# Diagonal blocks of a decayed Gram matrix stored once, and turned on chip for one of two scan directions

## The chip, the core and the metric

The kernel runs on one NeuronCore of a Trainium2 chip. A core has five engines that work at the same time: TensorE (PE in the profile; its weight loads are the row PEld), VectorE (DVE), ScalarE (ACT), GpSimd (POOL) and SyncE (SP), which here only issues DMAs. Each engine runs its own list of instructions strictly in order, and an instruction that waits for a semaphore holds up everything behind it on that engine. The metric is the device time of one whole execution in microseconds (us).

## The reference, cut to what matters

The program is one layer of a diffusion trunk over 2048 latent and 256 context tokens. An input projection feeds two token mixers: a gated delta rule that runs over the sequence in both directions (4 heads, key width 128, reference chunks of 64 tokens), and windowed attention. Both results are gated, projected, merged and projected once more.

The change touches the delta rule. For each chunk and head the reference builds a strictly lower triangular matrix and inverts one plus it:

```python
kb = kc * bc[..., None]
a_mat = jnp.where(strict, jnp.einsum('nbhik,nbhjk->nbhij', kb, kc) * decay, 0.0)
t_mat = lax.linalg.triangular_solve(a_mat, eye, left_side=True, lower=True, unit_diagonal=True)
...
o_f, s_f = _gdn_chunked(q, k, v, g[:, :, 0], beta[:, :, 0], s0_f, with_output)
o_b, s_b = _gdn_chunked(rev(q), rev(k), rev(v), rev(g[:, :, 1]), rev(beta[:, :, 1]), s0_b, with_output)
```

The second call runs on reversed tokens. So both directions use the same products of keys with keys, once in the lower and once in the upper triangle, each with its own decay and beta.

## The kernel before

The kernel works on 18 chunks of 128 tokens (2 of context, 16 latent; `LAT(j)` is chunk 2 + j). All big products are made of three matmuls each, since both operands are split into a high and a low half. The program is written in loops, and a planner orders the instructions of each engine by priority and by a simulation of the timeline; priority follows the order in which the program is written, except where `tc.high_priority` or `tc.issue_after` say otherwise. The order on each engine is then fixed: at run time a late DMA is waited for, and nothing overtakes it.

The stages, in the order of the profile:

1. Norm of the inputs and the small projections (to about 150 us).
2. `qkv(ORDER, ...)`: the projections v (m = 8 to 11), then k (m = 4 to 7), each in five segments: 256 context tokens and four times 512 latent tokens. `conv` applies the short convolution, and `finish` (L591) makes what the delta rule needs. For k, `finish` transposes the segment (L606), builds the Gram matrix of each chunk (L615), multiplies it with a table of decays `dt` that holds the forward decay in one triangle and the backward one in the other (L617, tile `p`), and spills blocks of 64 x 64 to DRAM through `spill_blocks` (L584). The backward direction (d = 1) reads `p` as it is. For the forward direction (d = 0) PE transposes each chunk of `p` against the identity (L629), ACT copies the result out of PSUM (L631, tile `pt`), and three more DMAs spill it. The tiles `p`, `pt`, the decays' `dt` and `qs` share the tag `o` with two buffers.
3. `qkv([0, 1, 2, 3], ...)`: the projection q, with the attention's queries beside it (from about 445 to 627 us).
4. `gates(range(24), (2, 3))`: 48 units of 24 matmuls, over the latter half of the tokens. Their order is fixed because the tiles `hh2` and `hh3` must be free before the scan can take their memory. Beside it, on DVE, `base` (L731) inverts the diagonal blocks of 8 heads-and-blocks times 8 chunks per direction at once: partition p holds one 64 x 64 block, forward blocks in partitions 0 to 63, backward ones in 64 to 127. It loads `N` (L745) and the betas `nb` (L744), multiplies (L748, L750), eliminates with 62 pairs of instructions per set (L758, L760), and stores (L770). There are two such sets: set 0 with the chunks that the scan needs first, set 1 with the others. A smaller one, `base4`, takes the last two chunks. `mod_gate` (L212) runs here too: 16 blocks of a weight are loaded into `wmg` (two buffers, L220), scaled by ACT (L221) and added up by POOL (L223).
5. `scan`: 18 steps, both directions side by side. `merge` (L999) loads the inverted diagonal blocks (`mx`, L1018) and the off-diagonal block (`moff`, L1020) of a chunk and completes the inverse of the whole 128 x 128 block with two rounds of 64 x 64 products. `chain` carries the state. Matmuls of `gates(range(24), (1, 0))` fill PE between them.
6. `attention`, `project` and the last projection (from about 1340 us to the end).

In `merge`, for the forward direction, the first product takes the block `moff` and the second half of the transposed inverse (L1037); DVE multiplies the result with beta into `y0` (L1041); the second product takes that and the first half of the inverse (L1044).

## Time and profile before

| what | us |
|---|---|
| median of 3 runs | 1994.18 (1990.22 to 1997.75) |
| the profiled execution | 1992.9 |
| its span, first to last instruction | 1991.2 |
| k segments, first Gram transposition to last (L629) | 300.5 to 435.9 |
| base, first to last elimination step (L758) | 647.2 to 949.8 |
| scan, first to last product with the inverse (L1115) | 920.7 to 1297.2 |

A row of the profile such as `L617 DVE TENSOR_TENSOR p<-gps,dtl x36: 423/690/693` names the line, the engine, the operation, the tile written and those read, the count, and the shortest, median and longest duration in ns. A row of the waits such as `DVE p L617 <- DMA dtl<-Dsp: 9.0, 5, 2.9` says that DVE stood for 9.0 us in all, 5 times, at most 2.9 us, in front of the instruction of line 617, and that a DMA ended it. `PEld` in front of a wait is the weight load's row; a `q` behind an engine's name is its sequencer, which also issues DMAs.

### The profile page before, as it was taken

What the parts mean: (1) busy time and instruction counts of PE and PEld (TensorE: products, weight loads), DVE (VectorE), ACT (ScalarE), POOL (GpSimd) and SP (SyncE); (2) the same over time, 40 slices, a digit from 0 to 9 for tenths busy, and PEclk for the clock granted to TensorE, in tenths of its full rate; (3) what the DMA queues carried; (4) which work ended last, traced back from release to release, by engine and by line L of the source; (5) the groups of instructions that cost most, each with busy time, mean ns of one, the idle gap of its engine ahead of it and who ended that gap; (6) DMA issues with size and microseconds to landing.
All of it is one profiled execution on the core that took longest, in us unless ns stands there. A gap on an engine that the chain in (4) does not pass through costs nothing. (4 is left out here: it accounts for less than half of the span.)

```text
span 1991.2 us, 32088 instructions
## 1 busy us (share of the span) xinstructions
PE 1917.4 (96%) x10947; PEld 1605.6 (81%) x10947; DVE 1502.1 (75%) x2869; ACT 802.6 (40%) x1994; POOL 692.1 (35%) x768
## 2 busy tenths in 40 slices
PE   7999999989999999999999999999989999999998
PEld 4888888779998787877888888788778887877786
DVE  6979766668776999999677776536686878747888
ACT  5755545554443323111222233225665656532221
POOL 2742211235542202004222234323555443420675
PEclk9999999999999999999999999999999999999999
DMA  7552226765547633528977877674455655455454
GB/s 263 173 142 87 91 89 161 195 157 175 151 134 196 170 106 116 145 89 237 230 232 225 240 212 207 178 216 146 143 176 171 185 161 164 119 173 190 141 169 135
DMA packets 387703, 333.12 MB, mean 167 GB/s; under 512 B 83992, under 2 KB 307536, under 8 KB 386900
## 3 DMA queue, kind: packets, MB, share of 16 engines
q1 hardware_dynamic: 352244, 288.60, 50.1%
q10 hardware_dynamic: 35296, 42.48, 6.1%
q8 instruction: 87, 1.43, 0.3%
q14 instruction: 76, 0.62, 0.1%
HBM read 220.28 MB, written 109.13 MB: 165 GB/s over the span
## 5 line engine op out<-in xcount | busy, mean ns | idle before, releaser
L535 PE MATMUL rps<-hh,wh 128*128 128x512 f32 x768 | 309.3, 403 | 3.7 <-DVE rt L829 2.5
L537 PE MATMUL rps<-hh,wl 128*128 128x512 f32 x768 | 307.6, 401 | 0.0
L536 PE MATMUL rps<-hl,wh 128*128 128x512 f32 x768 | 307.5, 400 | 0.0
L574 DVE SCALAR_TENSOR_TENSOR cacc<-y,cw,cacc 128x512 f32<-128x512 f32 (+1 forms) x224 | 164.0, 752 | 22.2 <-ACT cacc L572 18.3
L535 PEld LDWEIGHTS rps<-hh,wh 128*128 128x128 f32 x768 | 145.3, 189 | 39.4 <-DVE rt L829 3.3
L535 PE MATMUL lps<-hh,wh 128*128 128x512 f32 (+1 forms) x448 | 171.8, 384 | 0.3 <-ACT y L645 0.3
L536 PE MATMUL lps<-hl,wh 128*128 128x512 f32 (+1 forms) x448 | 171.5, 383 | 0.0
L537 PEld LDWEIGHTS rps<-hh,wl 128*128 128x128 f32 x768 | 145.2, 189 | 32.6
L536 PEld LDWEIGHTS rps<-hl,wh 128*128 128x128 f32 x768 | 145.5, 189 | 31.9
L537 PE MATMUL lps<-hh,wl 128*128 128x512 f32 (+1 forms) x448 | 171.0, 382 | 0.0
L961 DVE TENSOR_TENSOR pl<-pt,ph 128x512 fp32r<-128x512 f32 x156 | 105.4, 685 | 42.9 <-ACT ph L959 42.1
L959 ACT CAST ph<-pt 128x512 fp32r<-128x512 f32 x156 | 90.2, 585 | 110.2 <-PE pt L957 77.0
L827 ACT ACTIVATE rt<-rps 128x512 f32<-128x512 f32 x96 | 57.3, 597 | 185.0 <-PE rps L537 169.0
L933 DVE CUSTOM_DVE_ANT_0 pr<-sc,band,sk 128x640 f32<-128x640 f32 (+1 forms) x128 | 106.6, 862 | 32.1 <-PE sc L929 16.2
L943 POOL TENSOR_SCALAR pr<-pr,sm 128x640 f32<-128x640 f32 (+1 forms) x128 | 99.7, 802 | 56.5 <-DVE sm L941 39.3
L760 DVE TENSOR_TENSOR N<-N,btmp 128x62 f32<-128x62 f32 (+30 forms) x124 | 116.7, 941 | 3.0
L758 DVE TENSOR_TENSOR btmp<-N 128x62 f32<-128x62 f32 (+30 forms) x124 | 116.4, 939 | 3.1
L935 ACT ACTIVATE pr<-pr,sm 128x640 f32<-128x640 f32 (+1 forms) x128 | 104.0, 815 | 20.5 <-DVE sm L933 20.4
L246 DVE TENSOR_TENSOR wl<-wr,wh 128x512 fp32r<-128x512 f32 x120 | 92.4, 783 | 24.4 <-POOL wh L245 22.1
L1247 PE MATMUL pps<-yh,wph 128*128 128x512 f32 x256 | 105.6, 414 | 4.7 <-DVE tb L1258 2.5
L245 POOL TENSOR_SCALAR wh<-wr 128x512 fp32r<-128x512 f32 x72 | 48.8, 692 | 169.8 <-PE lps L536 97.1
L1248 PE MATMUL pps<-yl,wph 128*128 128x512 f32 x256 | 101.8, 399 | 0.0
(378 smaller groups left out, 5025.4 us busy)
## 6 DMA issues: line engine op xcount, KB each, us to landing
wr<-in_w_in_dram SPq DMA_DIRECT2D x120, 256.0 KB
kw<-Ksp SPq DMA_DIRECT2D x28, 384.0 KB
x<-vsp SPq DMA_DIRECT2D x36, 256.0 KB
k<-ksp SPq DMA_DIRECT2D x34, 256.0 KB
kT<-kTsp SPq DMA_DIRECT2D x34, 256.0 KB
wm<-in_w_mod_dram SPq DMA_DIRECT2D x16, 512.0 KB
xt<-in_x_dram SPq DMA_DIRECT2D x16, 512.0 KB
dtl<-Dsp SPq DMA_DIRECT2D x32, 256.0 KB
```

What stands on the lines that cost most here:

```text
L535: T.matmul(ps, lhsT=wh[:, k], rhs=xh[:, k], start=k == 0, stop=False)
L536: T.matmul(ps, lhsT=wh[:, k], rhs=xl[:, k], start=False, stop=False)
L537: T.matmul(ps, lhsT=wl[:, k], rhs=xh[:, k], start=False, stop=k == kt - 1)
L574: V.scalar_tensor_tensor(a, y[:, t:t + n], cw[:, m, t:t + 1], a, op0=ALU.mult, op1=ALU.add)
L758: V.tensor_tensor(tv, A[:, m + 1:, m].unsqueeze(2).to_broadcast([h1 + n, r, m]), A[:, m, 0:m].unsqueeze(1).to_broadcast([h1 + n, r, m]), o ...
L760: V.tensor_tensor(A[:, m + 1:, 0:m], A[:, m + 1:, 0:m], tv, op=ALU.add)
L933: V.tensor_tensor_reduce(s_, ps[:, o:768], band[:, b0:b0 + W + 256], -0.125, sk[:, 1, hd:hd + 1], ALU.add, ALU.min, sm[:, h, 1:2])
L935: S.activation(s_, s_, AF.Exp, scale=-1.0, bias=sm[:, h, 1:2], accum_out=sm[:, h, 2:3])
L943: G.tensor_scalar(p[:, h, :W + 256], p[:, h, :W + 256], sm[:, h, 3:4], 1.0, op0=ALU.mult, op1=ALU.mult)
L961: V.tensor_tensor(pl, pt, f32(ph), op=ALU.subtract)
L1247: T.matmul(ps, lhsT=wh[:, k, ms], rhs=hs[k], start=k == 0, stop=False)
L1248: T.matmul(ps, lhsT=wh[:, k, ms], rhs=ls[k], start=False, stop=False)
```

## The change

The diagonal blocks are stored once, as `p` has them, in one DRAM array `Nsp` in place of one per direction. The off-diagonal blocks of both directions are cut from `p` too, so the forward one is now stored the other way round and in partitions 0 to 63. PE's transposes of `p`, the copy `pt` and its spills go, except for the last two chunks of each head, whose forward diagonal blocks go to a small array `N4sp` for `base4`.

In front of the inversion the forward blocks are turned on chip. Set 0 loads all its forward blocks into a tile `u` (in the buffer that set 1's `N` takes afterwards), and three engines copy it with rows and columns exchanged: DVE 32 of the 64 columns, ACT 16, POOL 16. Set 1 is turned in eight pieces of 8 rows, each loaded into one buffer `ut` and copied by POOL. These loads and copies are now written in front of the gates of stage 4 and without the `issue_after` on the last convolution; the multiplications and the elimination stay where they were. `wmg` has one buffer in place of two.

In `merge` the forward direction's two products change places: DVE multiplies the loaded block with beta at once, the first product takes that and the first half of the inverse, ACT copies the result (in place of DVE's multiplication), and the second product takes it and the transposed half `W`.

```diff
-    Nsp = [dscr(f"Nsp{d}", [NC, H, 2, 64, 64]) for d in range(2)]
+    Nsp = dscr("Nsp", [NC, H, 2, 64, 64])
+    N4sp = dscr("N4sp", [2, H, 2, 64, 64])
...
-                wm = pool.tile([128, 512], F32, name="wmg", bufs=2)
+                wm = pool.tile([128, 512], F32, name="wmg", bufs=1)
...
-    def spill_blocks(d, t, c0, nn, h):
+    def spill_diag(dst, t, h):
         for b in range(2):
             r = slice(b * 64, b * 64 + 64)
-            dma(Nsp[d][c0:c0 + nn, h, b].rearrange("c r i -> r c i"), t[r, :, r])
-        dma(offsp[d][c0:c0 + nn, :, h].rearrange("c r i -> r c i"), t[64:128, :, 0:64])
+            dma(dst[:, h, b].rearrange("c r i -> r c i"), t[r, :, r])
+
+    def spill_blocks(t, c0, nn, h):
+        spill_diag(Nsp[c0:c0 + nn], t, h)
+        for d, (r, i) in enumerate(((slice(0, 64), slice(64, 128)), (slice(64, 128), slice(0, 64)))):
+            dma(offsp[d][c0:c0 + nn, :, h].rearrange("c r i -> r c i"), t[r, :, i])
...
-                spill_blocks(1, p, c0, nn, h)
+                spill_blocks(p, c0, nn, h)
...
-        if 4 <= m < 8:
-            pps = psum("gps", [128, 4, 128])
-            for j in range(nn):
-                T.transpose(pps[:, j], p[:, j], ident)
-            pt = pb.tile([128, 4, 128], F32, name="pt", tag="o")[:, :nn]
-            S.copy(pt, pps[:, :nn])
-            spill_blocks(0, pt, c0, nn, h)
+        if 4 <= m < 8 and c0 + nn == NC:
+            pps = psum("gps", [128, 2, 128])
+            for j in range(2):
+                T.transpose(pps[:, j], p[:, nn - 2 + j], ident)
+            pt = pb.tile([128, 4, 128], F32, name="pt", tag="o")[:, :2]
+            S.copy(pt, pps)
+            spill_diag(N4sp, pt, h)
...
+    def base_load(npool, fr, bk, turn):
+        N = npool.tile([128, 64, 64], F32, name="N")
+        nb = npool.tile([128, 64], F32, name="nb")
+        upper = [(slice(i0 * 8, i0 * 8 + 8 * k), Nsp[c:c + k].rearrange("c h b r i -> (c h b) r i")) for i0, c, k in runs(fr)]
+        turn(N, upper)
+        for d, chunks in ((0, fr), (1, bk)):
+            for i0, c, k in runs(chunks):
+                p0 = d * 64 + i0 * 8
+                dma(nb[p0:p0 + 8 * k], brT[c:c + k, d * 4:d * 4 + 4].rearrange("c h (b t) -> c (h b) t", b=2))
+                if d:
+                    dma(N[p0:p0 + 8 * k], Nsp[c:c + k].rearrange("c h b r i -> (c h b) r i"))
+        return N, nb
+
+    def turn_whole(pool):
+        def turn(N, upper):
+            u = pool.tile([128, 64, 64], F32, name="N")
+            for p, src in upper:
+                dma(u[p], src)
+            for copy, q in ((V.tensor_copy, slice(0, 32)), (S.copy, slice(32, 48)), (G.tensor_copy, slice(48, 64))):
+                copy(N[0:64, :, q], u[0:64, q].rearrange("p j r -> p r j"))
+        return turn
+
+    def turn_pieces(pool):
+        def turn(N, upper):
+            for q in range(0, 64, 8):
+                u = pool.tile([64, 8, 64], F32, name="ut", bufs=1)
+                for p, src in upper:
+                    dma(u[p], src[:, q:q + 8])
+                G.tensor_copy(N[0:64, :, q:q + 8], u.rearrange("p j r -> p r j"))
+        return turn
...
-    def base(si, npool, pool, fr, bk):
+    def base(si, N, nb, pool, fr, bk):
...
-            dma(N[p0:p0 + 16], Nsp[d][c:c + 2].rearrange("c h b r i -> (c h b) r i"))
+            dma(N[p0:p0 + 16], (N4sp, Nsp[c:c + 2])[d].rearrange("c h b r i -> (c h b) r i"))
...
     with tc.tile_pool(name="gate", bufs=1, reuse_waits="tile") as gp:
+        prepared = [base_load(bs, *SETS[0], turn_whole(bs2)), base_load(bs2, *SETS[1], turn_pieces(gp))]
         gates(list(range(24)), (2, 3), behind(4, mod_gate(gp, ones)), by_act=True)
...
         with tc.issue_after(last_conv[0].ins):
-            for _ in base(si, np_, bs2, fr, bk):
+            for _ in base(si, *prepared[si], bs2, fr, bk):
                 pass
...
-            dma(off[64:128], offsp[d][c])
+            r = slice(d * 64, d * 64 + 64)
+            dma(off[r], offsp[d][c])
...
         y0, y1 = offs[0], pool.tile([128, H, 64], F32, name="my1")
+        V.tensor_tensor(y0[0:64], y0[0:64], brb[0][0:64], op=ALU.mult)
...
-        in_step([lambda h: T.matmul(yps[0][0:64, h, 0:64], lhsT=offs[0][64:128, h], rhs=W[64:128, h, 64:128],
+        in_step([lambda h: T.matmul(yps[0][0:64, h, 0:64], lhsT=y0[0:64, h], rhs=Xs[0][0:64, h, 0:64],
                                     start=True, stop=True),
...
-        V.tensor_tensor(y0[0:64], yps[0][0:64, :, 0:64], brb[0][0:64], op=ALU.mult)
+        S.copy(y0[64:128], yps[0][0:64, :, 0:64])
...
-        in_step([lambda h: T.matmul(eps_[0][0:64, h, 0:64], lhsT=Xs[0][0:64, h, 0:64], rhs=y0[0:64, h],
+        in_step([lambda h: T.matmul(eps_[0][0:64, h, 0:64], lhsT=y0[64:128, h], rhs=W[64:128, h, 64:128],
                                     start=True, stop=True),
```

33 lines of the change are left out of this document (11 added, 22 removed).

## The prediction, made before the change was run

> **What bounds the kernel now.** I read the busy times of the engines by stage first.
>
> ```profile
> core 0: us, PE busy (x) PEld busy (x) DVE busy (x) ACT busy (x) POOL busy (x), PEclk, DMA share, GB/s
> 300.00:350.00 50.00, 50.00 (x286) 42.63 (x285) 32.76 (x60) 27.51 (x92) 4.99 (x4) 1.00 0.65 161
> 350.00:400.00 50.00, 47.57 (x277) 39.82 (x276) 34.77 (x67) 25.45 (x86) 13.88 (x16) 1.00 0.78 198
> 400.00:445.00 45.00, 39.19 (x272) 34.91 (x270) 31.58 (x72) 24.19 (x81) 14.31 (x13) 1.00 0.61 155
> 445.00:627.00 182.00, 181.25 (x1257) 165.18 (x1256) 137.70 (x318) 83.54 (x251) 87.43 (x103) 1.00 0.51 156
> 627.00:896.00 269.00, 266.48 (x1135) 212.10 (x1134) 247.52 (x292) 63.58 (x108) 34.20 (x26) 0.99 0.49 134
> 896.00:1300.00 404.00, 395.52 (x2891) 343.42 (x2889) 292.69 (x691) 104.41 (x338) 135.07 (x206) 0.99 0.77 220
> ```
>
> PE is the bound in each of these stages, at full clock in the first four rows. In 350 to 445 us it stands for 2.43 + 5.81 = 8.2 us. In the stage of the gates and of `base` (627 to 896) it stands for 2.5 us of 269; DVE is nearly full too (247.5), so I look at who needs DVE there:
>
> ```profile
> L758 DVE TENSOR_TENSOR btmp<-N x124: 212/1022/1828, 647.2 to 949.8; 128x62 f32<-128x62 f32 x4, 128x122 f32<-128x122 f32 x4, 128x180 f32<-128x180 f32 x4, 128x236 f32<-128x236 f32 x4
> L770 SPq DMA_DIRECT2D Xsp<-N x4: 512/548/590, 803.7 to 953.6; - x4
> L1018 SPq DMA_DIRECT2D mx<-Xsp x64: 573/607/2607, 898.3 to 1196.0; - x64
> ```
>
> `base` stores set 0 at 803.7 and the scan first reads such a block at 898.3: 94 us to spare. Set 1 is stored at 953.6 and first needed at step 8 of the scan, whose 18 steps fill the 404 us of the last row above (22 us each): at 898 + 8 x 22 = 1074. So the inversion is not on the path; the scan begins when the 48 gate units are through. Their pace:
>
> ```profile
> 859.73 0.39 PE L535 MATMUL rps<-hh,wh 128*128 128x512 f32 x1
> ...
> 886.33 0.39 PE L535 MATMUL rps<-hh,wh 128*128 128x512 f32 x1
> ```
>
> 114 matmuls lie between these starts, 26.60 / 114 = 0.233 us each; 48 x 24 x 0.233 = 268 us is the whole stage. Whatever PE saves before 627 us moves everything behind it forward by as much, as long as nothing new stops PE.
>
> **The change, part by part.** *The transposes in the k stage.*
>
> ```profile
> L629 PE MATMUL gps<-ident,p x72: 270/272/303, 300.7 to 435.9; 128*128 128x128 f32 x72
> 327.70 0.60 PE L629 MATMUL gps<-ident,p 128*128 128x128 f32 x4
> PE gps L629 <- DVE p L617: 2.7, 4, 1.5
> PE gps L629 <- DVE y L647: 2.2, 1, 2.2
> PE tmps L373 <- ACT y L645: 1.7, 1, 1.7
> PE gps L629 <- DVE y L650: 0.8, 1, 0.8
> ```
>
> Of 72 transposes 8 stay (two per head): 64 go. Four of them take 0.60 us with 0.27 for the last alone, so each follows the other by 0.11 us: 64 x 0.11 = 7.0 us of PE. In front of them PE stood for 2.7 + 2.2 + 0.8 = 5.7 us: it reaches the transpose before DVE has made `p`, and in order it cannot pass. With the transposes gone nothing on PE reads `p` in this stage except the 8 that stay. Bounds 0 (the next matmul waits for the same lateness) to 5.7; I take 4, nearer to the upper end, because what is next is mostly a dense product that needs only weights and `hh`.
>
> ACT and the queues of the same step:
>
> ```profile
> L631 ACT COPY pt<-gps x20: 372/584/610, 301.6 to 436.9; 128x512 f32<-128x512 f32 x16, 128x256 f32<-128x256 f32 x4
> ACT pt L631 <- DMA offsp<-pt: 8.1, 5, 3.6
> L588 SPq DMA_DIRECT2D Nsp<-pt x40: 574/598/818, 302.0 to 438.6; - x40
> L617 DVE TENSOR_TENSOR p<-gps,dtl x36: 423/690/693, 296.3 to 627.7; 128x512 f32<-128x512 f32 x32, 128x256 f32<-128x256 f32 x4
>   DMA dtl<-Dsp: 23.1, 18
> DMA packets 58987, 26.52 MB, mean 166 GB/s; under 512 B 31064, under 2 KB 56279, under 8 KB 58972
> ```
>
> ACT loses 16 of 20 copies (16 x 0.58 = 9.3 us) and most of an 8.1 us wait for the buffer of `pt`. Behind that copy on ACT stand the copies `y` that free PSUM for PE; the 1.7 us that PE waited for `y` L645 are of this kind: bounds 0 to 1.7, I take 1. SP loses 40 spills of diagonal blocks and gains 8, 32 x 0.60 = 19 us of its issue time; the off-diagonal ones stay 40. DVE waited 23.1 us for decays `dtl` queued behind those spills. All this feeds DVE and ACT, which are not full here, so beyond the 1 us I count nothing, and the rest stands as the rival of a larger gain. Sum of the k stage: 7.0 + 4 + 1 = 12, bounds 7.0 to 7.0 + 8.2 (all of PE's idle time) = 15.2.
>
> *The turning of set 0.*
>
> ```profile
> DVE N L748 <- DMA N<-Nsp: 6.1, 1, 6.1
> DVE N L750 <- DMA N<-Nsp: 6.1, 2, 4.2
> L748 DVE TENSOR_TENSOR N<-N,nb x8: 416/810/1210, 634.5 to 655.0; 64x256 f32<-64x256 f32 x2, 64x512 f32<-64x512 f32 x2, 64x768 f32<-64x768 f32 x2, 64x1024 f32<-64x1024 f32 x2
> L750 DVE TENSOR_TENSOR N<-N,nb x8: 422/821/1227, 643.6 to 660.3; 64x256 f32<-64x256 f32 x2, 64x512 f32<-64x512 f32 x2, 64x768 f32<-64x768 f32 x2, 64x1024 f32<-64x1024 f32 x2
> L1042 ACT COPY my<-myp x18: 369/369/371, 912.2 to 1285.4; 64x256 f32<-64x256 f32 x18
> L1014 POOL COPY mx<-x x8: 620/629/992, 1223.1 to 1274.8; 64x256 f32<-64x256 f32 x8
> L245 POOL TENSOR_SCALAR wh<-wr 128x512 fp32r<-128x512 f32 x72 | 48.8, 692 | 169.8 <-PE lps L536 97.1 <-PE rps L536 56.9 <-DMA wr<-in_w_in_dram 15.2
> ```
>
> DVE copies 2048 elements per partition; 1024 took 1.21 us, so about 2.4. ACT: 256 took 0.37 and 512 took 0.58, so 1024 about 1.0. POOL: the only strided copy here takes 0.63 for 256, so 1024 takes 2.5. Forward blocks landed by 634.5 and were multiplied; DVE then stood until 643.6 for the backward ones. Turning (2.5) and the four multiplications (3.3) end at 640.3, inside that wait. Cost 0; if the cover were gone, 2.5 us on a chain with 94 us to spare. No bound of it reaches PE unless an eviction (`rt`, L829) behind a waiting copy is late by more than the three PSUM banks hold, 3 x 24 x 0.233 = 17 us.
>
> *The eight pieces of set 1 and the single buffer of `wmg`.* All are on SP, in front of or between the loads of gate weights (L241) and the stores.
>
> ```profile
> SPq L220 <- POOL gacc L223: 14.2, 6, 6.9
> SPq L241 <- DVE wl L246: 12.4, 7, 4.7
> ACT wh L243 <- DMA wr<-in_w_in_dram: 8.8, 4, 5.4
> 674.88 2.09 SPq L220 DMA_DIRECT2D wmg<-in_w_mod_dram  x2
> 679.49 0.72 ACT L221 ACTIVATE wmg<-wmg,silc 128x512 f32<-128x512 f32 x1 [3.92 <-DMA wmg<-in_w_mod_dram]
> ```
>
> The second of those two issues ends at 676.97 and ACT has the data at 679.49: 2.5 us to land. A piece of half that size lands, is copied by POOL (512 elements strided: 2 x 0.63 = 1.26 us) and only then frees `ut` for the next load: 0.34 + 2.5 + 1.26 = 4.1 us, eight times 33 us if SP stands at each. A gate unit pair covers 48 x 0.233 = 11.2 us, and weights are loaded one pair ahead. So the bounds for the pieces are 0 and 33 - 11 = 22 us of PE. I take 1, because SP already stood 14.2 + 12.4 us in this stretch and ACT 8.8 us for weights while PE lost 2.5 us. `wmg` with one buffer makes 16 rounds of 2.5 + 0.7 + 1.5 us, which 269 us hold easily; its waits go with the same 1 us.
>
> [...]
>
> *The merge.* Matmuls stay as many. DVE's multiplication (L1041) moves in front, ACT gets a copy of 0.37 us per step (18 x 0.37 = 6.6 us, on an engine busy 104 of 404 us: 0). The new wait: DVE now reads `moff` straight from its DMA, with the state's instructions queued behind it, and PE waits for those.
>
> ```profile
> L1041 DVE TENSOR_TENSOR moff<-myp,br x18: 405/406/410, 913.7 to 1286.6; 64x256 f32<-64x256 f32 x18
> 1040.20 0.47 SPq L1020 DMA_DIRECT2D moff<-offsp  x1
> 1045.00 0.49 PE L1027 MATMUL mtp<-ident,mx 128*128 128x128 f32 x3
>   DMA x<-vsp: 31.2, 18
> ```
>
> The nearest row is POOL's first use of `x` (L1102), which waited 31.2 us over 18 times: upper bound 31, lower bound 0, or -1.5 where PE no longer waits for L1041. I take 1: `moff` is issued 4.8 us ahead of the transposes in the quoted step, and it is not needed sooner.
>
> **The sum.** 1992.9 - 12 + 1 + 1 = 1982.9 us, against the profiled execution, which lies 1.3 us under the median shown. I say 1983.
>
> **Rivals.** *The gain is lost on the way.* PE's next instruction waits for the same DVE and ACT work, and a planner that orders everything anew gives some back. For it: DVE is 65 to 70% busy in the k stage and PE's idle time there is mixed. Against it: in 300 to 350 us PE is never idle, so its own work is what ends last. Only some of the 7.0 us then arrive: 1992.9 - 3 = 1990.
>
> *A larger gain.* All 8.2 us of idle time go: 1992.9 - 15.2 = 1978. For it: SP's 19 us, ACT's 17 and the spills' packets, of which 32 x 256 = 8192 go (64 rows of 4 chunks each), out of 31064 small ones. Against: part of the waits is for `conv`, which stays. [...]
>
> *SP is held by the pieces, and the gates' weights come late* (slower). Place: 630 to 700 us, SP in order, L241 behind the loads into single buffers. Price: 22 us of PE for the pieces, up to 36 with three rounds of `wmg` (3 x 4.7 us) among them; I take 25, 1992.9 - 12 + 1 + 25 = 2007. It decides from the point where a weight load is issued over 11.2 us late. For it: 33 us of holding in a stretch that already has 27. Against: the planner knows of these waits and only their excess over its own times counts.
>
> **How the numbers follow.** What a measurement here can tell from no change is about 0.5%, 10 us: under 1984.2 is faster, over 2004.2 slower. Chances: forecast 0.50 (its own range 1977 to 1989), gain lost 0.26, larger gain 0.13, slower 0.11. Of the forecast's half, 0.31 lies under 1984.2; with 0.13 of the larger gain and 0.02 of the lost one, faster has 0.46. The slower rival and the tail of the merge's wait leave 0.11 over 2004; same has 0.43. The range that holds 8 in 10: 1975 (upper bound of the k stage, the merge's -1.5 and some spread) to 1997 (gain lost, with part of the pieces' hold).
>
> **What would show it.** In the profile after: L629's successor with 8 matmuls; PE without waits for `p` in the k stage and the q stage beginning some 12 us sooner; the gates' stage still about 269 us long, with PE idle under 4 us; the base's first elimination at the same distance from the stage's beginning; few us of DVE waiting for `moff`. Wrong if the k stage is shorter by less than 7 us, if PE waits for weights between the first gates and the pieces' last copy, or if the scan is longer than 404 us by more than a few.

## The result and the profile after

The changed kernel takes 2015.75 us (median of 4 runs, 2013.49 to 2017.79), the kernel before 1994.99 us beside it (1990.22 to 1997.75): 1.0106 times as long, with a 95% interval of 1.0082 to 1.0131. The forecast was 1983 us. The profiled execution took 2017.79 us, its span is 2016.1 us, 24.9 us more than the 1991.2 of the span before.

Busy time by stage, kernel after (columns as in the prediction; the stages begin where the same work begins, so the borders differ from those before):

```profile
300.00:350.00 50.00, 50.00 (x276) 42.51 (x274) 32.28 (x62) 26.02 (x90) 6.18 (x6) 1.00 0.60 152
350.00:400.00 50.00, 45.45 (x269) 38.65 (x268) 35.82 (x70) 25.43 (x89) 14.79 (x15) 1.00 0.71 183
400.00:439.00 39.00, 34.01 (x226) 30.00 (x225) 29.19 (x69) 19.28 (x68) 14.76 (x13) 1.00 0.62 165
439.00:621.00 182.00, 181.21 (x1254) 164.99 (x1254) 136.61 (x317) 82.25 (x249) 86.28 (x101) 1.00 0.50 154
621.00:902.00 281.00, 270.52 (x1136) 214.44 (x1135) 252.44 (x286) 64.89 (x110) 51.23 (x34) 0.98 0.47 128
902.00:1320.00 418.00, 404.01 (x2882) 345.75 (x2881) 298.29 (x697) 110.39 (x349) 133.94 (x208) 0.99 0.74 210
```

The stage from 439 us on begins 6 us sooner, not 12. PE stands for 10.5 us of the gates' row, where it stood for 2.5, and the scan's row is 14 us longer than the 404 of before.

For a table of stages I take three marks that every kernel has: the first matmul of a gate, the scan's first load of an inverted block (`mx<-Xsp`, issued when the 48 gate units are through), and attention's last score. Instructions by tile, columns: duration min/median/max in ns, first and last start in us. Kernel after:

```profile
L536 PE MATMUL rps<-hh,wh x768: 388/394/793, 611.5 to 1444.7; 128*128 128x512 f32 x192
L1045 SPq DMA_DIRECT2D mx<-Xsp x64: 573/605/2642, 904.7 to 1221.8; - x64
L954 PE MATMUL sc<-kw,qT x128: 276/336/525, 1367.9 to 1763.5; 128*128 128x384 f32 x112, 128*128 128x256 f32 x16
```

The same, kernel before (its `mx<-Xsp` row, 898.3, stands in the prediction):

```profile
L535 PE MATMUL rps<-hh,wh x768: 388/394/789, 617.0 to 1418.5; 128*128 128x512 f32 x192
L927 PE MATMUL sc<-kw,qT x128: 276/336/522, 1342.8 to 1738.7; 128*128 128x384 f32 x112, 128*128 128x256 f32 x16
```

| us | gates begin | gates' stage | scan and attention | rest | span |
|---|---|---|---|---|---|
| before | 617.0 | 281.3 | 840.4 | 252.5 | 1991.2 |
| after | 611.5 | 293.2 | 858.8 | 252.6 | 2016.1 |
| difference | -5.5 | +11.9 | +18.4 | +0.1 | +24.9 |

So the k stage gave 5.5 us; the gates' stage took 11.9 back and the scan with attention 18.4 more. Scan and attention are kept together because both plans put the remaining gate units beside them, some more in the one, some more in the other; the sum of work is the same.

**The k stage.** Waits of PE between 290 and 450 us, and the transposes that stay, kernel after:

```profile
PE zt L612 <- DVE cacc L577: 5.4, 4, 2.1
PE gps L635 <- DVE p L623: 2.4, 2, 1.8
L635 PE MATMUL gps<-ident,p x8: 270/272/328, 328.0 to 428.8; 128*128 128x128 f32 x8
```

The 64 transposes are gone. The 5.7 us in front of them are not: PE now waits 5.4 us for the convolution's result (`cacc`) one step sooner, and 2.4 us in front of two of the eight transposes that stay.

**The gates' stage.** Timeline of the loads (SP) and of DVE, kernel after: start, duration, engine, line, and in brackets the idle time before it and what ended it.

```profile
620.94 0.35 SPq L722 DMA_DIRECT2D N<-Nsp  x1
623.93 0.45 SPq L722 DMA_DIRECT2D N<-Nsp  x1
629.68 0.60 SPq L730 DMA_DIRECT2D N<-Nsp  x1
```

```profile
633.31 2.09 DVE L776 TENSOR_TENSOR N<-N,nb 64x768 f32<-64x768 f32 x2
635.43 0.69 DVE L855 SCALAR_TENSOR_TENSOR rt<-rt,rps 128x512 f32<-128x512 f32 x1
643.20 2.10 DVE L732 COPY N<-N 64x2048 f32<-64x2048 f32 x1 [7.08 <-DMA N<-Nsp]
645.33 3.59 DVE L774 TENSOR_TENSOR N<-N,nb 64x256 f32<-64x256 f32 x3
648.84 3.38 DVE L247 TENSOR_TENSOR wl<-wr,wh 128x512 fp32r<-128x512 f32 x2
652.15 0.67 DVE L855 SCALAR_TENSOR_TENSOR rt<-rt,rps 128x512 f32<-128x512 f32 x1
```

The planner puts the load of the blocks to be turned (L730, tile `u`) behind both loads of the backward blocks. It is issued at 629.68 and landed at 643.2, when the backward blocks had been through their multiplications for 8 us. DVE stands before it for 7.1 us, then turns, multiplies, and makes `wl`; the next eviction of a gate (`rt`, L855) comes 16.7 us after the one before. Waits in this stage (611 to 902 us), kernel after: engine, tile, line, what was waited for, us in total, times, longest.

```profile
PE rps L536 <- DVE rt L855: 10.5, 4, 4.2
...
ACT wmg L222 <- DMA wmg<-in_w_mod_dram: 57.9, 14, 9.9
...
ACT wh L244 <- DMA wr<-in_w_in_dram: 15.2, 6, 4.9
ACT N L732 <- DMA N<-Nsp: 9.6, 1, 9.6
```

The same rows of PE and ACT, kernel before (617 to 896 us):

```profile
PE rps L535 <- DVE rt L829: 2.5, 1, 2.5
ACT wmg L221 <- DMA wmg<-in_w_mod_dram: 20.7, 10, 4.1
```

PE waits 8.0 us more for evictions than before, two thirds of the stage's 11.9 us. Most of the rest goes with the granted clock, by an estimate from the records. Busy time and clock between 650 and 700 us, kernel before and kernel after:

```profile
650.00:700.00 50.00, 47.48 (x197) 37.69 (x196) 47.32 (x60) 14.83 (x25) 11.45 (x9) 0.97 0.56 156
650.00:700.00 50.00, 40.85 (x154) 31.80 (x155) 48.26 (x58) 11.80 (x22) 22.22 (x16) 0.91 0.52 146
```

Behind the one pause of PE in the stage before (2.5 us) the trace has 3.4 us at half clock (a granted share of 0.50). After, there are three such pieces, from 653.7, 681.0 and 698.0 us, behind pauses of 4.2, 2.9 and 2.7 us. In the first of them the gates' matmuls follow each other by 0.43 us, behind it by 0.23:

```profile
654.55 0.63 PE L538 MATMUL rps<-hh,wl 128*128 128x512 f32 x1
654.97 0.63 PE L536 MATMUL rps<-hh,wh 128*128 128x512 f32 x1
...
657.33 0.39 PE L536 MATMUL rps<-hh,wh 128*128 128x512 f32 x1
657.56 0.40 PE L537 MATMUL rps<-hl,wh 128*128 128x512 f32 x1
```

If half of each piece is lost, that is 5.1 us in place of 1.7 (an estimate from these records). With the 8.0 us it makes 11.4 of the 11.9. ACT, which evicts and casts weights here, now stands 57.9 us for `wmg` and 9.6 for `u`; the detail above is of the first pause, and what share each cause has in the other two is not shown.

**Scan and attention.** DVE waits in the scan (895 to 1330 us), kernel after; the kernel before has no such row:

```profile
DVE moff L1061 <- DMA moff<-offsp: 22.4, 10, 8.6
```

This row made my first theory: the merge costs through DVE, which stands in front of a late load with the scan's instructions behind it.

### The profile page after: what moved, and what is told of

Read it like the earlier page. It is cut to its first block, busy times and chain, and to the rows that moved or that the text cites. A ratio compares the mean times of both kernels' runs of the same rounds, so it can differ in the third digit from the quotient of the medians.

```text
span 2016.1 us, 31836 instructions
## 1 busy us (share of the span) xinstructions
PE 1923.0 (95%) x10883; PEld 1603.5 (80%) x10883; DVE 1511.3 (75%) x2870; ACT 803.8 (40%) x1997; POOL 706.9 (35%) x777
## 5 line engine op out<-in xcount | busy, mean ns | idle before, releaser
L536 PE MATMUL rps<-hh,wh 128*128 128x512 f32 x768 | 310.6, 404 | 12.7 <-DVE rt L855 10.5
L1278 PE MATMUL pps<-yh,wpl 128*128 128x512 f32 x256 | 100.9, 396 | 0.0
```

Source lines behind the costliest of these rows:

```text
L536: T.matmul(ps, lhsT=wh[:, k], rhs=xh[:, k], start=k == 0, stop=False)
L1278: T.matmul(ps, lhsT=wl[:, k, ms], rhs=hs[k], start=False, stop=k == 3)
```

## The experiments

All comparisons are with the kernel before on the same chip, which took 1987.7 to 1990.8 us in these sessions. Stages by the marks above, from one profiled execution each; the ratio decides on the whole and the stages tell where. The profiled execution lies within 6 us of its kernel's median, but for e4 (11.5 us under it) and e15 (7.8 us over it); the kernel before's, 1992.9 us, is 2 to 5 us over the medians of these sessions. So a few us in one row for a stage mean little.

| kernel | gates begin | gates' stage | scan and attention | rest | ratio of times |
|---|---|---|---|---|---|
| before | 617.0 | 281.3 | 840.4 | 252.5 | 1 |
| after | 611.5 | 293.2 | 858.8 | 252.6 | 1.0106 |
| e1 merge alone | 623.2 | 281.6 | 844.5 | 256.5 | 1.0093 [1.0066, 1.0120] |
| e4 turning alone | 618.0 | 290.8 | 839.5 | 251.0 | 1.0111 [1.0071, 1.0150] |
| e5 k stage alone | 611.5 | 285.0 | 846.8 | 252.9 | 1.0046 [1.0023, 1.0070] |
| e9 one `wmg` buffer alone | 616.7 | 287.6 | 848.9 | 255.6 | 1.0105 [1.0076, 1.0133] |
| e3 after, no turning | 611.6 | 287.1 | 851.7 | 251.5 | 1.0100 [1.0075, 1.0125] |
| e6 after, old merge | 613.6 | 292.9 | 855.8 | 250.8 | 1.0129 [1.0102, 1.0155] |
| e2 after, product held | 612.5 | 293.0 | 858.8 | 250.1 | 1.0155 [1.0126, 1.0183] |
| e7 after, `moff` early | 611.6 | 292.9 | 859.5 | 253.8 | 1.0166 [1.0140, 1.0191] |
| e12 e7, product held | 611.8 | 291.9 | 844.9 | 252.3 | 1.0087 [1.0062, 1.0112] |
| e16 e1, early and held | 623.0 | 282.9 | 844.9 | 253.8 | 1.0090 [1.0069, 1.0111] |
| e8 turned by POOL | 610.0 | 289.4 | 859.3 | 255.3 | 1.0150 [1.0125, 1.0175] |
| e11 turned by ACT | 612.2 | 294.8 | 853.4 | 254.6 | 1.0137 [1.0115, 1.0160] |
| e13 two `wmg` buffers | 611.9 | 300.1 | 855.5 | 253.9 | 1.0187 [1.0160, 1.0213] |
| e14 inversion held | 612.3 | 293.6 | 859.2 | 255.7 | 1.0157 [1.0132, 1.0183] |
| e15 e12, e13, e14 together | 613.8 | 297.0 | 858.5 | 252.5 | 1.0141 [1.0113, 1.0169] |
| e10 transposes twice | 620.1 | 281.4 | 838.0 | 252.6 | 1.0032 [1.0015, 1.0050] |
| e17 inversion late | 616.9 | 290.7 | 850.2 | 250.3 | 1.0102 [1.0061, 1.0142] |
| e18 directions swapped | 618.8 | 281.8 | 853.8 | 251.2 | 1.0083 [1.0059, 1.0108] |

### One part at a time

**e1, the merge alone.** The kernel before with the edits in `merge`, and both off-diagonal blocks spilled from `p`:

```diff
-        dma(offsp[d][c0:c0 + nn, :, h]..., t[64:128, :, 0:64])
+        if d:
+            for dd, (r, i) in enumerate(((slice(0, 64), slice(64, 128)), (slice(64, 128), slice(0, 64)))):
+                dma(offsp[dd][c0:c0 + nn, :, h]..., t[r, :, i])
```

> The kernel before with the new merge alone: the forward off-diagonal block is cut from p instead of pt, DVE multiplies it with beta as soon as it is loaded, ACT copies the first product. Transposes, pt and the inversion stay as before. Theory A (the scan is longer because DVE waits for the DMA of moff at the front of each merge): the stretch from the first to the last product with the inverse grows from 372 us by 10 to 20 us, and the time is 2005 to 2015. Rival B (the scan is longer only because its start and the second inversion set came late, so DVE is shared for longer): the stretch stays at 372 and the time within 4 us of before, 1995.

2007.46 us, inside theory A's range. But the place is not A's: of the span's 14.6 us only 4.1 lie in scan and attention, although DVE waits for `moff` more than in the kernel after, and the stretch that theory A names grew by 6 us (927.8 to 1306.1, in place of 920.9 to 1292.9), not by 10 to 20; 6.2 lie ahead of the gates and 4.0 behind attention, which I did not follow up. Its row, kernel e1:

```profile
DVE moff L1036 <- DMA moff<-offsp: 26.5, 12, 5.1
```

**e2, the product held behind the first transposes.**

```diff
-        V.tensor_tensor(y0[0:64], y0[0:64], brb[0][0:64], op=ALU.mult)
+        with tc.issue_after(first_tp.ins):
+            V.tensor_tensor(y0[0:64], y0[0:64], brb[0][0:64], op=ALU.mult)
```

> The changed kernel, with DVE's multiplication of moff in merge held back until PE has made the transposes of the forward block, by when moff has landed. Theory A: DVE's wait of 22 us for moff goes, the scan's stretch falls from 392 to 372 to 380 us, the time from 2016 to about 2000. Rival B: the stretch stays near 392 and the time near 2015.

2018.72 us, but nothing was tested: DVE's product already stood behind these transposes in the order, every engine's list is the same as in the kernel after, and the wait stayed (20.7 us). It serves as a second measurement of the kernel after. The two stages agree within 0.2 us; the ratios, 1.0106 and 1.0155, show that two sessions can differ by 0.5% with the same lists.

**e3, the kernel after without turning**: the forward blocks are loaded as stored, so what is inverted for them is the transposed block.

```diff
-        turn(N, upper)
+        for p, src in upper:
+            dma(N[p], src)
```

> The changed kernel without the turning: the forward blocks are loaded straight into N, in the stored orientation (so the forward inverses are those of other matrices); everything else as changed, the merge too. Theory C (the turning holds DVE in front of the evictions of the gates' stage): PE's waits for rt in 611 to 903 us go from 10.5 to under 3 us, the stage from 292 to about 281 us, the time from 2016 to about 2004. Rival D (the stage is longer because the loads were moved in front of the gates, turned or not): the stage stays within 3 us of the changed kernel's.

2008.44 us, between the two. The gates' stage gives 6.1 of its 11.9 us back, scan and attention 7.1 of 18.4, in an execution 4.9 us under the median. PE's waits for `rt` stay at 7.1 us, where theory C had under 3. The rest is there without any turning.

**e4, turning alone.** The kernel before with `base_load`, `turn_whole`, `turn_pieces` and one buffer for `wmg`; the k stage and the merge are the old ones.

```diff
-        N = npool.tile([128, 64, 64], F32, name="N")
+        prepared = [base_load(bs, *SETS[0], turn_whole(bs2)), base_load(bs2, *SETS[1], turn_pieces(gp))]
...
-                wm = pool.tile([128, 512], F32, name="wmg", bufs=2)
+                wm = pool.tile([128, 512], F32, name="wmg", bufs=1)
```

> The kernel before with the turning alone: the forward blocks are read from the backward direction's array and turned as in the change, with the loads in front of the gates and one buffer for wmg; transposes, pt, spills and merge as before. Theory C: the gates' stage is 10 to 13 us longer and the time 2005 to 2008. Rival E (the turning hurts only because the k stage ended earlier and the loads met other transfers): the stage is under 4 us longer and the time under 2000.

2012.58 us; the profiled execution was its fastest, 2001.07. The gates' stage has +9.5 us, scan and attention nothing (-0.9). Theory C has the place right and is too low in time; where the other 11.5 us of the median lie, no trace shows.

**e5, the k stage alone.**

```diff
-        turn(N, upper)
+        for p, src in upper:
+            dma(N[p], src)
...
-            dma(off[r], offsp[d][c])
+            dma(off[64:128], offsp[d][c])
```

This is the kernel after with the first edit of e3, the merge of before, and two buffers for `wmg`. The loads for the inversion still stand in front of the gates, as in the kernel after.

> The change's k stage alone (transposes, copies and spills gone, two extra diagonal chunks stored turned, two buffers for wmg again). The turning is left out (the forward direction's diagonal blocks are inverted as they are stored) and the merge is the one of before, which here reads the untransposed off-diagonal blocks, so the output differs. Theory A (turning and merge are what costs): about 6 us faster than before, the 5.5 us by which the gates began sooner in the kernel after; gates' stage 279 us long, TensorE idle between gates and attention 42 to 44 us. Rival B (any new plan of the scan around the k stage's shorter work costs some 15 us, whatever the merge does): 2000 us or more, TensorE idle between gates and attention above 52 us.

1997.57 us, 9 us slower where theory A said 6 faster. The 5.5 us are gained, then 3.7 are lost in the gates' stage and 6.4 in scan and attention, whose code is the one of before. Rival B is too high with 2000, but right in kind: the loss needs neither the turning nor the merge. What of the 3.7 us comes from the moved loads is not shown.

**e6, the kernel after with the old merge.** Its turning and its `wmg` stay as they are.

```diff
-            dma(off[r], offsp[d][c])
+            dma(off[64:128], offsp[d][c])
...
-        V.tensor_tensor(y0[0:64], y0[0:64], brb[0][0:64], op=ALU.mult)
...
-        S.copy(y0[64:128], yps[0][0:64, :, 0:64])
+        V.tensor_tensor(y0[0:64], yps[0][0:64, :, 0:64], brb[0][0:64], op=ALU.mult)
```

> The kernel after with the merge of before in place of the new one (it reads the untransposed off-diagonal blocks, so the output differs). Theory A (the new merge costs 13 to 17 us of TensorE between gates and attention): 1998 to 2003 us, that idle time back at 42 to 44 us, gates' stage still 288 to 291 us long. Rival B (the turning costs as much as it did when made alone, 25 us, and the merge nothing on top): 2010 to 2016 us.

2014.08 us. Without the new merge scan and attention still take 855.8 us, 15.4 more than before. Theory A, that the merge is what the scan loses, falls here.

**e9, one buffer for `wmg`, and nothing else.**

```diff
-                wm = pool.tile([128, 512], F32, name="wmg", bufs=2)
+                wm = pool.tile([128, 512], F32, name="wmg", bufs=1)
```

> The kernel before with one buffer in place of two for wmg, and nothing else; no work is added or removed, but the planner then puts 22% of TensorE's matmuls from the scan on into another order. Theory P (what the merge and the scan lose is the price of another order of the scan, which any edit ahead of it can bring): 4 to 20 us slower, TensorE idle between gates and attention above 46 us in place of 42.4. Rival M (the order is worth nothing by itself, only the edited merge and the turning cost): within 4 us of before, idle time 41 to 45 us.

2012.01 us: this one word costs about as much as the whole change. ACT's row in the gates' stage, kernel e9:

```profile
ACT wmg L221 <- DMA wmg<-in_w_mod_dram: 49.5, 13, 11.4
```

Against 20.7 with two buffers: ACT stands at each round, with evictions and casts behind it. The gates' stage is 6.3 us longer, and PE waits 7.1 us for evictions there. The 8.5 us in scan and attention are as theory P says, since no instruction there has changed but its place.

### The wait for `moff`

**e7, the load a whole step sooner** (and the copied product in a tile of its own):

```diff
+    def load_off(pool, cs):
+        off = pool.tile([128, H, 64], F32, name="moff", bufs=3)
...
+                if st + 2 < NC:
+                    offs.append(load_off(pool, [orders[d][st + 2] for d in range(2)]))
-                W = merge(pool, [orders[d][st + 1] for d in range(2)])
+                W = merge(pool, [orders[d][st + 1] for d in range(2)], offs[st + 1])
```

> The kernel after, with the off-diagonal blocks of each step loaded a whole step sooner (one tile for both directions, three buffers, a tile of its own for the copied product). Theory A (VectorE standing in front of the late load of moff is what the merge costs): the wait of 22 us for moff falls under 5, TensorE idle between gates and attention from 57 to 42 to 46 us, time 2000 to 2005 us. Rival B (the new merge costs by its longer chain, product, copy and second product, and by the order it brings for the rest): the wait is gone, the idle time stays above 53 us, time 2011 to 2018 us.

2020.7 us, and the wait is longer. Kernel e7, DVE between 905 and 1353 us:

```profile
DVE moff L1064 <- DMA moff<-offsp: 27.5, 11, 5.0
```

The loads were issued earlier, and the planner moved the product up behind them (2.3 to 10.1 us behind its load's issue, where it was 3.3 to 13.8). I take it that the planner puts an instruction that reads straight from a DMA where it believes that the data has landed; it then waits for what the planner misjudged, wherever the load stands.

**e12, e7 with the product behind the other direction's**, which waits for PE's transposes in any case:

```diff
-        V.tensor_tensor(y0[0:64], y0[0:64], brb[0][0:64], op=ALU.mult)
-        V.tensor_tensor(y1[64:128], ...)
+        y1_done = V.tensor_tensor(y1[64:128], ...)
+        with tc.issue_after(y1_done.ins):
+            V.tensor_tensor(y0[0:64], y0[0:64], brb[0][0:64], op=ALU.mult)
```

> The kernel e7 (moff loaded early), and VectorE's product of moff put behind the product of the other direction, which waits for TensorE's transposes anyway. Theory A (VectorE standing before the load is what costs): its wait for moff, 27.5 us in e7, falls under 5, TensorE's idle time between gates and attention to 42 to 48 us, time 2003 to 2008 us. Theory P (the order of the scan as a whole costs, not this wait): the wait falls, the idle time stays above 53 us, time 2013 us or more.

2008.25 us. The row for `moff` is gone from DVE's waits, and scan and attention take 844.9 us, 14.6 less than in e7; the ratios differ by 0.8%, 16 us. That is close to theory A's numbers, but the order of the scan is another one too.

**e16, the same two edits on the merge alone (e1).**

```diff
+        y1_done = V.tensor_tensor(y1[64:128], ...)
+        with tc.issue_after(y1_done.ins):
+            V.tensor_tensor(y0[0:64], y0[0:64], brb[0][0:64], op=ALU.mult)
```

> The new merge alone (as e1), with moff loaded a step earlier and its product put behind the other direction's (as in e12). Theory A (the merge costs through VectorE's wait for moff, 26.5 us in e1): the wait falls under 5, TensorE idle between gates and attention from 55 to 42 to 46 us, time within 4 us of before (e1 was 18 us slower). Rival B (its longer chain or another order of the scan costs): 2000 us or more.

2006.96 us, as slow as e1 (2007.46). The wait is gone here too, and scan and attention take 844.9 us against 844.5: nothing gained. Rival B. So taking away the same wait of 26 to 28 us went with 14.6 us in one plan and with nothing in another. Its price can't be read from its row.

### The gates' stage

**e8, the first set turned by POOL alone**, one copy of 4096 elements a row.

```diff
-            for copy, q in ((V.tensor_copy, slice(0, 32)), (S.copy, slice(32, 48)), (G.tensor_copy, slice(48, 64))):
-                copy(N[0:64, :, q], u[0:64, q].rearrange("p j r -> p r j"))
+            G.tensor_copy(N[0:64], u[0:64].rearrange("p j r -> p r j"))
```

> The kernel after, with the first set's blocks turned by GpSimd alone (one copy of 4096 elements a row in place of shares on VectorE, ScalarE and GpSimd). Theory A (VectorE's and ScalarE's evictions stand behind their share of the turning, which waits for the load of u): VectorE's wait of 7 us and ScalarE's of 10 us before the turning are gone, the gates' stage 280 to 284 us in place of 290.6, time 2006 to 2010 us. [...]

2017.18 us; the gates' stage 289.4, longer than theory A's 280 to 284. The waits of DVE and ACT before the turning are gone and the stall stays, for another reason. Timeline of POOL and DVE, kernel e8:

```profile
641.44 7.48 POOL L731 COPY N<-N 64x4096 f32<-64x4096 f32 x1 [18.68 <-DMA N<-Nsp]
643.72 7.42 DVE L247 TENSOR_TENSOR wl<-wr,wh 128x512 fp32r<-128x512 f32 x2 [9.61 <-ACT wh L244]
```

The same instruction of DVE, kernel before, gates' stage:

```profile
L246 DVE TENSOR_TENSOR wl<-wr,wh x46: 677/684/1782, 637.5 to 886.3; 128x512 fp32r<-128x512 f32 x46
```

Two of them take 7.42 us in place of 1.37, and 5.2 us of that lie beside POOL's copy. DVE also stood 9.6 us for ACT's cast before this, and ACT 11.0 us in front of `wmg`.

**e11, all turning on ACT**; PE's order is the one of the kernel after.

```diff
+            for q in (slice(i, i + 16) for i in range(0, 64, 16)):
+                S.copy(N[0:64, :, q], u[0:64, q].rearrange("p j r -> p r j"))
...
-                G.tensor_copy(N[0:64, :, q:q + 8], u.rearrange("p j r -> p r j"))
+                S.copy(N[0:64, :, q:q + 8], u.rearrange("p j r -> p r j"))
```

> The kernel after with all of the turning's copies on ScalarE, none on VectorE or GpSimd (TensorE's order is the same as in after). Theory A (GpSimd's strided copies stretch VectorE's instructions, and those hold TensorE up): no VectorE instruction of the set's beginning is stretched, the gates' stage 281 to 284 us in place of 290.6, the same as in the kernel without turning (282.9 to 284.7), time 2006 to 2010 us. Rival B (the copies stand in front of the evictions wherever they run, because the turned tile arrives late): ScalarE's evictions stall instead and the stage stays at 287 us or more.

2019.84 us, the gates' stage 294.8: no better without POOL's copies, as rival B said, though ACT has them to do instead. DVE now waits for ACT's copies, and PE for evictions as before. Kernel e11, 612 to 903 us:

```profile
PE rps L536 <- DVE rt L855: 11.2, 2, 5.7
```

```profile
DVE N L774 <- ACT N L732: 12.2, 4, 8.5
```

**e13, two `wmg` buffers in the kernel after.** To make room, the second set's pieces are two rows each, 32 of them.

```diff
-                wm = pool.tile([128, 512], F32, name="wmg", bufs=1)
+                wm = pool.tile([128, 512], F32, name="wmg", bufs=2)
-            for q in range(0, 64, 8):
+            for q in range(0, 64, 2):
```

> The kernel after with two buffers for wmg again (the turned pieces of the second set are two rows each in place of eight, 32 of them, so that both fit); TensorE's order is the same as in after, matmul for matmul. Theory A (ScalarE's wait for the one wmg buffer, 58 us against 21 before, holds its casts and evictions up, and these TensorE): ScalarE's wait falls to 20 to 28 us, the gates' stage from 290.6 to 283 to 286 us, the time to 2007 to 2011 us. Rival B (the wait is idle time that ScalarE has anyway): the stage stays at 288 us or more, the time within 3 us of after.

2025.6 us, the slowest of all. ACT's wait for `wmg` falls to 39.4 us, but another takes its place. ACT and SP in the gates' stage, kernel e13:

```profile
ACT wh L244 <- DMA wr<-in_w_in_dram: 92.7, 20, 16.0
```

```profile
SPq L741 <- DMA ut<-Nsp: 33.5, 25, 3.0
```

ACT waited 15.2 us for gate weights in the kernel after. SP stands 33.5 us before loads into the one small buffer, with the weights' loads behind it. This is the prediction's slower rival, at 32 pieces; at eight it didn't occur. The run doesn't tell what the second buffer alone is worth in the kernel after.

**e14, turning and inversion held behind the gates' seventh unit.**

```diff
+        def beside():
+            yield from behind(3, ())
+            prepared[0][2]()
+            prepared.append(base_load(bs2, *SETS[1], turn_pieces(gp)))
+            yield
+            yield from mod_gate(gp, ones)
...
-        with tc.issue_after(last_conv[0].ins):
+        with tc.issue_after(rt_done[3].ins):
```

`prepared[0][2]` makes the first set's copies, `rt_done[m]` is DVE's first eviction of gate m.

> The kernel after with the first set's turning, and all that the base inversions do on VectorE, put behind the gates' seventh unit (about 650 us); the loads stay where they were. Theory A (VectorE stands before loads that are 7 and 6 us late while TensorE's evictions queue behind it): VectorE's and ScalarE's waits before the turning are gone, the gates' stage 281 to 285 us in place of 290.6, the time 2006 to 2011 us. Rival B (the stall only moves to a later unit, by the stretched VectorE instructions): the stage stays at 288 us or more.

2021.43 us, the gates' stage 293.6, rival B. Kernel e14, 612 to 903 us:

```profile
PE rps L536 <- DVE rt L858: 13.4, 3, 10.9
```

The stall at 648 us shrinks and one of 10.9 us at 675 us takes its place. The turning was not held: load and copies come as in the kernel after, and DVE stands 9.1 us before them again. The multiplications were, and of both sets at once. Instructions on `N` by tile, kernel e14:

```profile
L730 SPq DMA_DIRECT2D N<-Nsp x1: 545/545/545, 630.6 to 630.6; - x1
L734 DVE COPY N<-N x1: 2083/2083/2083, 644.0 to 644.0; 64x2048 f32<-64x2048 f32 x1
L777 DVE TENSOR_TENSOR N<-N,nb x8: 418/945/2222, 666.5 to 695.3; 64x256 f32<-64x256 f32 x2, 64x512 f32<-64x512 f32 x2, 64x768 f32<-64x768 f32 x2, 64x1024 f32<-64x1024 f32 x2
L779 DVE TENSOR_TENSOR N<-N,nb x8: 422/1373/2030, 667.0 to 680.3; 64x256 f32<-64x256 f32 x2, 64x512 f32<-64x512 f32 x2, 64x768 f32<-64x768 f32 x2, 64x1024 f32<-64x1024 f32 x2
```

They fill DVE from 666.5 to 683 us, so the evictions of the gates at 665.9 and 685.1 us lie 19.3 us apart.

**e15, the three mends together**: e12's `load_off` and held product, e13's two buffers, e14's `beside`.

```diff
+        with tc.issue_after(y1_done.ins):
+            V.tensor_tensor(y0[0:64], y0[0:64], brb[0][0:64], op=ALU.mult)
...
+                wm = pool.tile([128, 512], F32, name="wmg", bufs=2)
...
+        with tc.issue_after(rt_done[3].ins):
```

> All three mends in the kernel after: moff loaded early with its product held (as in e12), two buffers for wmg (as in e13), turning and inversion held (as in e14). If the three costs add up: e12's 2008 less 5 to 7 for wmg and 4 to 8 for the held inversion, 1993 to 1999 us, TensorE idle in the gates' stage 6 to 9 us. Rival (a scan planned anew costs beside them): 2003 us or more.

2015.71 us, no better than the kernel after; scan and attention are back at 858.5 us (in an execution 7.8 us over the median) although the product of `moff` is held as in e12. The costs don't add up.

### The order of the scan

**e10, the old transposes issued twice.**

```diff
-            for j in range(nn):
+            for j in [*range(nn)] * 2:
                 T.transpose(pps[:, j], p[:, j], ident)
```

> The kernel before with each of the k stage's transposes of p issued twice (64 more matmuls of 0.11 us, 7 us). Theory P (another order of the scan costs by itself): the k stage 6 to 8 us longer, and beyond that 4 us or more lost between gates and attention, 2000 to 2010 us in all. Rival M (only the added work costs): 6 to 8 us slower, 1994 to 1997 us, with idle time between gates and attention within 2 us of before's 42.4.

1997.63 us, 6 to 7 us slower, as the rival says. But the run does not test theory P: from the scan on, its order is the one of the kernel before. In the trace 12 of 6157 matmuls stand at another place, and none of the instructions of DVE, ACT and POOL. With the order the stretch stayed, too (838.0 us). 3.1 us are lost ahead of the gates; the profiled execution is 3.8 us under the median, so where the rest lies is not shown.

**e17, the inversion 20 us later in the kernel before.**

```diff
-        with tc.issue_after(last_conv[0].ins):
+        with tc.issue_after(rt_done[2].ins):
```

> The kernel before with the base inversions' work on VectorE put behind the gates' fifth unit, so that it starts and ends some 20 us later; nothing is turned, added or removed. Theory D (what the scan loses in the kernel after is VectorE's share of the second set's inversion, which ends at 971 us there in place of 951 and so reaches 69 us into the stages behind the gates in place of 55): the inversion ends at 968 to 976 us, TensorE idle between gates and the end of attention 12 to 18 us above before's 84.2, 2000 to 2008 us in all. Rival (its end is of no account, as forecast by 94 us of slack): idle time within 5 us of before's, 1988 to 1994 us.

2011.66 us. The stores of the two sets, kernels e17 and after:

```profile
L770 SPq DMA_DIRECT2D Xsp<-N x4: 487/547/2168, 822.6 to 987.5; - x4
```

```profile
L796 SPq DMA_DIRECT2D Xsp<-N x4: 481/540/597, 813.0 to 972.8; - x4
```

The second set comes later than in the kernel after. Scan and attention lose 9.8 us, between the two expectations, and the gates' stage 9.4 by a stall that has nothing to do with it: the planner moved the sums of `mod_gate` forward. The order of the scan changes as well, so the run can't tell the late inversion from the order; in e5 and e18, which lose in the scan too, the second set is stored at 951.4 and 956.9 us, about as before (953.6). Kernel e17:

```profile
PE gsum L227 <- POOL gacc L223: 11.1, 1, 11.1
```

**e18, the two directions of a scan step written in the other order.** They are alike and independent; no work and no dependence changes.

```diff
-            r = [chain(d, st, W[d]) for d in range(2)]
+            r = [chain(d, st, W[d]) for d in (1, 0)][::-1]
```

> The kernel before with the two directions' chains of a scan step written in the other order; they are independent of each other and alike, so no work and no dependence changes, and nothing ahead of the scan does, but 13% of TensorE's matmuls from the scan on stand in another order. Theory P (any other order of the scan costs): 5 us or more slower. Rival D (the order is of little account as long as VectorE's other work is the same): within 4 us of before.

2008.12 us, 18 us slower by the medians and 14.4 by the spans, 13.4 of them in scan and attention (853.8 against 840.4 us). Theory P. Busy time over scan and attention as one stretch, kernels before, after and e18, in this order:

```profile
898.00:1739.00 841.00, 816.10 (x5149) 694.78 (x5147) 591.33 (x1335) 342.93 (x870) 327.83 (x418) 0.99 0.65 191
```

```profile
905.00:1764.00 859.00, 826.57 (x5147) 699.28 (x5145) 596.29 (x1340) 350.76 (x888) 323.12 (x417) 0.99 0.63 187
```

```profile
901.00:1755.00 854.00, 825.18 (x5147) 699.75 (x5146) 592.61 (x1334) 344.29 (x870) 328.49 (x417) 0.99 0.64 188
```

The matmuls are as many, and DVE, ACT and POOL are as busy in e18 as before; the stretch is 13 us longer. PE's idle time accounts for 3.9 us of that (24.9 to 28.8), its busy time for 9.1. A part of this is the clock, which two digits hide: the trace has half clock for 13.7 us of the stretch before, 23.9 us in e18 and 20.5 us after, in pieces of 3.4 or 6.8 us that begin in a pause of PE or within 1.5 us of its end. If half of each piece is lost, e18 loses about 5 us more by it than the kernel before, and the kernel after 3.4 (estimates from these records). One such place in e18:

```profile
1004.00:1014.00 10.00, 6.29 (x41) 5.80 (x43) 7.33 (x22) 0.00 (x0) 4.12 (x6) 0.66 0.69 205
```

There is no one wait behind it. Among DVE's waits the one for POOL's half of the weights grew most, while others became shorter. Kernel before, 896 to 1343 us, and kernel e18, 898 to 1353 us:

```profile
DVE wl L246 <- POOL wh L245: 10.7, 8, 3.3
```

```profile
DVE wl L246 <- POOL wh L245: 30.0, 13, 7.8
```

Which feature of the old order made it good is open.

## Why the prediction was wrong, by its steps

**The k stage, 12 us: 5.5 came.** The 64 transposes are gone, and 7.0 us is about right as their work; but issuing them twice moved the gates only 3.1 us back, so some of them fill time in which PE would stand anyway. Of the 1 us for `y` 0.7 came (PE waits 1.0 us there in place of 1.7). The term of 4 us of waits was wrong: of the 5.7 us in front of the transposes nothing was won, since PE waits for `cacc` and `p` instead (7.8 us). My lower bound, that the next matmul waits for the same lateness, was the truth. The rival of a lost gain had this right, and only this.

**Turning set 0, cost 0: the cover wasn't there.** I let the forward blocks land first, as before (by 634.5), so that the turning hid in the wait for the backward ones. The new plan loads them last. The turning begins at 643.2, where I had the multiplications ended at 640.3. The condition under which I said that it would reach PE, an eviction queued behind a waiting copy for about 17 us, is what happened: evictions at 635.4 and 652.15. Durations were off as well, below. By runs, turning costs the gates' stage 3.2 us (e4 against e9) to 6.1 us (after against e3).

**Pieces and the `wmg` buffer, 1 us: mis-sized.** The pieces themselves did little, at eight. That 269 us "hold easily" 16 rounds counted the loop alone and not ACT, which carries out each round in order in front of PE's evictions. Alone it takes 6.3 us of the gates' stage, and the kernel with nothing but this edit is 1.05% slower.

**The merge, 1 us: the wait was seen, its price not.** DVE's wait for `moff` is 22.4 us, inside the bounds that I gave (to 31) and far from the 1 I took. That it is "issued 4.8 us ahead of the transposes" was a distance of the old order, in which no engine waited for that load. Yet the price isn't 22 us either: e6 without the new merge is 3.0 us better in scan and attention, e12 without the wait 13.9, and e16 no better than e1. All three also have another order.

**What the sum left out.** I took the scan as it was, 404 us, and shifted it. Its order was made anew in nearly every kernel above, and the order of before is a good one. e10, which keeps it, takes as long over scan and attention as before; of the others all but e4, in its fastest execution, take 4 to 19 us longer, some with no changed work there (e5, e9, e18). e18 shows that the order alone can cost 13 us. That this is the main part of the 18.4 us in the kernel after is inferred from e5, e6, e9 and e18 together; no run put the old order under the changed kernel. My rival of the lost gain said that "a planner that orders everything anew gives some back", and then priced it inside the k stage. Nor did the sum have a term for the clock: it counted a pause of PE by its length, and the half clock behind the pauses added, by the estimates above, about 3.4 us in the gates' stage and as much in scan and attention.

**The slower rival** came nearest with 2007 us, by luck. Its place was right: PE's three longer pauses begin at 648.7, 678.1 and 693.9 us. Its mechanism was not: SP stood 5.4 us before the pieces' buffer, and ACT waited no longer for gate weights (15.2 us, before 16.5).

None of the versions is faster than the kernel before.

## What to carry to other kernels

In a kernel ordered by a planner, an edit has two costs: its work, and the new order of everything behind it; measure the second with an edit that changes the order and no work, here a swap of two equal chains worth 0.8%, before believing a forecast of half as much. A load that arrives "in time" by the old profile does so only in the old order (DVE's wait for `moff`: none before, 22.4 us after), so for each instruction that newly reads from a DMA ask what stands behind it on its engine, and price that by the evictions PE needs. Count a buffer taken away as a wait in the middle of the in-order engine that uses it (ACT stood 49.5 us for `wmg` in e9, 20.7 before), not as a share of the stage.

## What was not expected of the hardware

Copies with rows and columns exchanged did not scale as I had assumed. Timeline, kernel after:

```profile
643.25 2.12 ACT L732 COPY N<-N 64x1024 f32<-64x1024 f32 x1 [9.56 <-DMA N<-Nsp]
643.29 3.86 POOL L732 COPY N<-N 64x1024 f32<-64x1024 f32 x1 [19.05 <-DMA N<-Nsp]
```

ACT took 2.12 us for 1024 elements, where I had 1.0 from packed rows; DVE 2.10 for 2048, where I had 2.4. POOL took 3.86 here, where I had 2.5, but 7.48 for 4096 in e8, which is 1.87 for each 1024; so the 3.86 is not the price of the exchange alone. It ran beside DVE's copy (643.20 to 645.30 us); what it would take alone no run shows.

Beside the longer pauses of PE the trace has pieces of half clock, which the forecast left out. In the kernel after, each of the six pauses over 2.4 us between 611 and 1764 us has 3.4 or 6.8 us at a granted clock of 0.50 beside it.

DVE's `wl`, 0.684 us at the median in the kernel before, took 7.42 us for two beside POOL's copy of 7.48 us in e8: POOL's copy ran from 641.44 to 648.92, DVE's pair from 643.72 to 651.14. Why the pair took longer no run isolates.
